# Multiplying half-seen blocks of probabilities at half width, and one group per head in a windowed attention

## Chip, cores and metric

The kernel runs on one core of a Trainium2 chip. The metric is the device time of one execution in microseconds. The engines are named as in the profile: PE is TensorE (PEld its weight loads), DVE is VectorE, ACT is ScalarE, POOL is GpSimd, and SP issues most of the transfers.

## What is computed

The reference is one layer of a decoder on 1024 tokens of width 1024: three attentions side by side, A, B and C, whose outputs are gated and merged, and then an MLP. What matters here is what each attention multiplies with the values:

```python
# A, per head: two softmaxes, their difference, all earlier keys
w = p[0] - lam * p[1]
return jnp.einsum('bhqk,bkhe->bqhe', w, v)
# B: a window of 128 keys, 8 heads, 2 key/value heads
mask = ((dist >= 0) & (dist < window)) & (k_pos >= 0)
o = jnp.einsum('bngrqk,bnkgd->bngrqd', p, vb)
# C: three softmaxes, of compressed keys, of selected blocks (here all), of a window of 512
out = g[..., 0:1] * o_cmp + g[..., 1:2] * o_sel + g[..., 2:3] * o_win
```

Tokens and keys are cut into tiles of 128, eight of each. In A and in the selected part of C, token tile t sees key tiles 0 to t; in B it sees t - 1 and t; in the window of C it sees t - 4 to t.

## The kernel before

Every product of two float32 matrices is made of float32r halves: a high part and a low part are split off by ACT (L90, the copy that rounds) and by DVE or POOL (L91, the difference), and TensorE multiplies two or three times with them (mm3, L114 to L120; head_values in B and C, L901 and L902).

The work of A, B and C is made from two streams. The fine stream is the attention itself. It works on items: in A one head and one pair of token tiles (2qb, 2qb+1), in B two heads and one pair, in C one head and one pair. An item has rows (logits on TensorE at L711, the minimum on DVE at L735, the exponential on ACT at L743, the scaling at L941 in B and L1046 in C) and groups. A group transposes blocks of probabilities on TensorE (L759) into one PSUM tile of 512 columns, splits them into ph and pl (pblocks, L745), and two groups later multiplies them with the values (values, for A, or head_values). All products of one item and head go into one PSUM tile, ac, 256 columns wide, 128 for each token tile; there is a single one of it. When the last product is in, ACT and DVE evict it (L907 and L908, tiles ot and ob; L889 in A), and the next head's first product waits for that.

The dense stream is the projection of the next head, the gates, or the first branch: long runs of 384 or 512 columns wide multiplies that need no attention result. The function mix lays the two streams into TensorE's order: each fine step returns an estimate of its TensorE time and of its DVE time, and dense steps are put in until the sum of TensorE's estimates has reached what DVE's are worth (PACE and STEP are the factors). The order on TensorE is the one so written; the other engines' orders are made by a scheduler.

A group holds two key tiles (in B one or two, see below), each for two token tiles, so four blocks of 128 columns. Where a key tile is seen by one token tile only, its other block is zero: POOL writes zeros into ph and pl (L756, L757) and the multiply runs over all 256 columns. The order of the key tiles within the tile is chosen (order, L772) so that the written blocks lie side by side. B's pairs have three key tiles from the second pair on, 2qb-1, 2qb and 2qb+1, which the kernel before handles as two groups per head: one of key tile 2qb-1 alone (one block and a zero block) and one of the other two.

Of the kernel before, what the change touches and what calls it, by code (L numbers as in the profile page):

```python
# [11 lines left out]
F32 = mybir.dt.float32  # L12
# [5 lines left out]
P = 128  # L18
# [57 lines left out]
class Kernel:  # L76
# [668 lines left out]
    def pblocks(self, blocks):  # L745

        nc, at = self.nc, self.at
        ph = at.tile([P, 512], F32R, name="ph", tag="ph", bufs=self.dist)
        pl = at.tile([P, 512], F32R, name="pl", tag="pl", bufs=self.dist)  # L750
        pt = self.tr()
        rows = blocks[0][0].shape[-1]
        used = sorted(o for _, o in blocks)
        for o in range(0, used[-1] + (2 * P if used[-1] % (2 * P) == 0 else P), P):
            if o not in used:
                nc.gpsimd.memset(ph[0:rows, o:o + P].bitcast(F32), 0.0)  # L756
                nc.gpsimd.memset(pl[0:rows, o:o + P].bitcast(F32), 0.0)  # L757
        for src, o in blocks:
            nc.tensor.transpose(pt[0:rows, o:o + P], src, self.ident)  # L759
        s = slice(used[0], used[-1] + P)  # L760
        assert used == list(range(s.start, s.stop, P))
        with self.tc.high_priority(offset=self.urgent):
            self.split(ph[0:rows, s], pl[0:rows, s], pt[0:rows, s])
        return ph, pl

    def group(self, prow, qb, kts, vis, values):

        out = {}
        see = [[j for j in range(2) if vis(2 * qb + j, kt)] for kt in kts]  # L770

        order = sorted(range(len(kts)), key=lambda i: (see[i] == [0], see[i] != [1]))  # L772
        blocks = [(i, j, (2 * x + j) * P) for x, i in enumerate(order) for j in see[i]]

        def tp():
            out["p"] = self.pblocks([(prow(j, kts[i]), o) for i, j, o in blocks])
            return 0.11 * len(blocks)

        def pv():
            ph, pl = out["p"]  # L780
            c = 0.0
            for i in range(len(kts)):
                s = slice(order.index(i) * 256, order.index(i) * 256 + 256)
                c += values(i, ph[:, s], pl[:, s])
            return c

        return tp, pv

    def items_a(self, h, sta):
        nc, at = self.nc, self.at  # L790
        bias = self.bias[:, h, :]
        for qb in range(4):
            pq = [None, None]
            box = {}
# [58 lines left out]
            def values(i, ph, pl, kt, qb=qb, box=box):  # L853
                if kt + i == 0:
                    box["ac"] = self.ac()
                self.mm3(box["ac"], sta["v"][:, kt + i, 0, :], sta["v"][:, kt + i, 1, :], ph, pl,
                         kt + i == 0, kt + i == 2 * qb + 1)
# [6 lines left out]
            groups = [self.group(lambda j, kt, pq=pq: pq[j][:, kt * P:(kt + 1) * P], qb, (kt, kt + 1),  # L864
                                 lambda t, kt: kt <= t, lambda i, ph, pl, kt=kt, values=values: values(i, ph, pl, kt))
# [28 lines left out]
    def head_values(self, box, dst, v, ph, pl, first, last):  # L894
# [6 lines left out]
        nc.tensor.matmul(ac, v, ph, start=first, stop=False)  # L901
        nc.tensor.matmul(ac, v, pl, start=False, stop=last)  # L902
# [9 lines left out]
    def items_b(self, g, sta):  # L912
        nc, at = self.nc, self.at
        bias = self.bias
        for qb, r0 in [(qb, r0) for qb in range(4) for r0 in (0, 2)]:
# [31 lines left out]
            kts = list(range(max(2 * qb - 1, 0), 2 * qb + 2))  # L947
            box = {}
            for i in range(2):
                def prow(j, kt, i=i, pq=pq):  # L950
                    p, k0 = pq[j]
                    return p[:, i, (kt - k0) * P:(kt - k0 + 1) * P]

                r = r0 + i
                dst = self.od[4 + 2 * g + r // 2, (r % 2) * 64:(r % 2) * 64 + 64, qb * 256:(qb + 1) * 256]
                for grp in ([kts] if len(kts) == 2 else [kts[0:1], kts[1:3]]):
                    def values(i, ph, pl, grp=grp, kts=kts, box=box, dst=dst):
                        kt = grp[i]
                        return self.head_values(box, dst, sta["v"][:, kt, :], ph, pl, kt == kts[0], kt == kts[-1])

                    groups.append(self.group(prow, qb, grp, lambda t, kt: t - 1 <= kt <= t, values))
            yield dict(rows=rows, groups=groups, end=[])

    def items_c(self, g, sta):
        nc, at = self.nc, self.at
        bias4 = self.bias
        for r in range(4):
            for qb in range(4):
# [82 lines left out]
                for j in range(2):  # L1051
# [13 lines left out]
                hv = lambda v, ph, pl, first, last, dst=dst, box=box: self.head_values(  # L1065
                    box, dst, v, ph, pl, first, last)
                blk = {}

                def tp_c(rows=rows, blk=blk):
                    blk["p"] = self.pblocks([(rows[j][0], j * P) for j in range(2)])  # L1070
                    return 0.22

                def pv_c(blk=blk, hv=hv):
                    ph, pl = blk["p"]
                    return hv(self.vct[:, g, :], ph[:, 0:256], pl[:, 0:256], True, False)

                groups = [(tp_c, pv_c)]
                for kt in range(0, 2 * qb + 2, 2):
# [3 lines left out]
                        lambda i, ph, pl, kt=kt, hv=hv: hv(sta["vs"][:, kt + i, :], ph, pl, False, False)))  # L1082
                for kt in range(max(2 * qb - 4, 0), 2 * qb + 2, 2):
# [3 lines left out]
                        lambda i, ph, pl, kt=kt, hv=hv, qb=qb: hv(sta["vw"][:, kt + i, :], ph, pl, False,  # L1087
                                                                  kt + i == 2 * qb + 1)))
# [500 lines left out]
```

## Time and profile before

| what | value |
|---|---|
| median of 3 runs | 2041.63 us (2040.56 to 2045.64) |
| profiled execution | 2045.69 us |
| its span | 2043.7 us, granted clock 0.98 |
| attention A, B, the two halves of C | 147 to 436, 436 to 558, 627 to 870, 917 to 1194 us |
| blocks of probabilities transposed (L759) | 792 of p, 64 of pc, in 280 evictions |
| multiplies into ac | 240 in A, 848 in B and C |
| memsets of ph and pl on POOL | 152 and 152 |

The span runs from the first to the last instruction; the execution's own time has 2.0 us around it. In a group of the profile stand the line, the engine, the operation, the tiles (out<-in), the shape and the count, then the busy time in us, the mean of one in ns, the engine's idle time just before them and what ended most of that. A matmul is pipelined with the next, so its length is not what it costs: the cost is the step from its start to the next one's. A line such as "POOL ph L756 <- PE ac L901" in the waits says which instructions waited for which, with the total, the number of times and the longest.

### The profile page before, as it was taken

How to read it: one execution, taken by the hardware profiler on the slowest of the kernel's cores; microseconds unless marked ns; L12 is line 12 of the kernel's file. 1: busy time of each engine (PE TensorE's matmuls, PEld its weight loads, DVE VectorE, ACT ScalarE, POOL GpSimd, SP SyncE). 2: the span in 40 equal slices, each digit the busy share in tenths (PEclk: the TensorE clock that was granted, in tenths of full speed). 3: DMA queues.
4: the chain of work that ended last, by engine and by line, in shares of the span. 5: the costliest groups of instructions: out<-in, count | busy, mean ns of one | idle time of the engine just before them, and what ended most of it. 6: DMA issues, size and time to landing. Idle time of an engine off the chain costs nothing. (4 is left out here: it accounts for less than half of the span.)

```text
span 2043.7 us, 30701 instructions
## 1 busy us (share of the span) xinstructions
PE 1901.7 (93%) x9838; PEld 1621.5 (79%) x9838; DVE 1423.4 (70%) x3231; ACT 1022.0 (50%) x2626; POOL 954.3 (47%) x1142
## 2 busy tenths in 40 slices
PE   7999888988799999999999899999899998999998
PEld 6888887888688888887888677787688886888876
DVE  6757777788848677648676755657755544889898
ACT  5456556666636555536555533335455544444331
POOL 4455355544352212162222227218444445789784
PEclk9999999999999999999999899999899998999999
DMA  5131022011211111212242456425444446355343
GB/s 218 51 104 52 4 55 59 26 38 37 87 28 61 56 52 51 72 33 91 68 147 77 159 198 204 147 93 161 172 167 160 144 145 247 119 167 163 124 144 114
DMA packets 122558, 219.49 MB, mean 107 GB/s; under 512 B 14420, under 2 KB 35412, under 8 KB 122396
## 3 DMA queue, kind: packets, MB, share of 16 engines
q1 hardware_dynamic: 120812, 211.75, 31.9%
q10 hardware_dynamic: 1584, 5.77, 0.9%
q8 instruction: 78, 1.28, 0.3%
q14 instruction: 84, 0.69, 0.1%
HBM read 156.59 MB, written 64.81 MB: 108 GB/s over the span
## 5 line engine op out<-in xcount | busy, mean ns | idle before, releaser
L91 POOL TENSOR_TENSOR wl<-wr,wh 128x512 fp32r<-128x512 f32 (+3 forms) x246 | 328.8, 1343 | 275.0 <-ACT wh L90 238.8
L90 ACT ACTIVATE wh<-wr 128x512 fp32r<-128x512 f32 (+3 forms) x258 | 150.3, 590 | 183.8 <-PE mm L119 124.1
L711 PE MATMUL sc<-st 128*128 128x256 f32 (+5 forms) x736 | 183.9, 344 | 25.9 <-ACT p L743 25.3
L90 ACT ACTIVATE ph<-tr 128x384 fp32r<-128x384 f32 (+3 forms) x280 | 138.4, 497 | 105.5 <-PE tr L759 87.0
L91 DVE TENSOR_TENSOR pl<-tr,ph 128x384 fp32r<-128x384 f32 (+3 forms) x280 | 155.8, 559 | 40.2 <-ACT ph L90 37.6
L756 POOL MEMSET ph<- 128x128 f32 x152 | 35.7, 235 | 291.3 <-PE ac L901 253.0
L711 PEld LDWEIGHTS sc<-st 128*128 128x128 f32 x736 | 122.8, 192 | 47.5 <-ACT p L743 38.8
L118 PE MATMUL mm<-hh,wh 128*128 128x512 f32 x384 | 158.8, 414 | 0.0
L120 PE MATMUL mm<-hh,wl 128*128 128x512 f32 x384 | 151.5, 395 | 0.0
L119 PE MATMUL mm<-hl,wh 128*128 128x512 f32 x384 | 151.4, 394 | 0.0
L119 PE MATMUL mm<-wl,wh 128*128 128x512 f32 x352 | 139.5, 396 | 9.4 <-POOL wl L91 9.4
L118 PE MATMUL mm<-wh 128*128 128x512 f32 x352 | 139.9, 398 | 8.2 <-DVE x L1471 5.3
L90 ACT ACTIVATE wh<-u 128x512 fp32r<-128x512 f32 x162 | 93.0, 620 | 106.3 <-PE mm L119 27.9
L759 PE MATMUL tr<-ident,p 128*128 128x128 f32 x792 | 129.2, 275 | 16.9 <-ACT o L889 7.8
L120 PE MATMUL mm<-wh,wl 128*128 128x512 f32 x352 | 139.1, 395 | 0.0
L743 ACT ACTIVATE p<-sc,mc 128x256 f32<-128x256 f32 (+5 forms) x200 | 106.7, 538 | 52.0 <-DVE mc L735 47.0
L901 PE MATMUL ac<-ph,st 128*128 128x256 f32 x392 | 109.8, 298 | 19.4 <-DVE ob L908 11.5
L91 POOL TENSOR_TENSOR wl<-s,wh 128x512 fp32r<-128x512 f32 x64 | 89.5, 1405 | 79.3 <-ACT wh L90 79.3
L118 PE MATMUL mm<-wh,hh 128*128 128x384 f32 (+1 forms) x320 | 117.0, 366 | 0.0
L91 DVE TENSOR_TENSOR wl<-u,wh 128x512 fp32r<-128x512 f32 x98 | 112.5, 1150 | 3.9 <-ACT wh L90 3.9
L902 PE MATMUL ac<-pl,st 128*128 128x256 f32 x392 | 106.5, 292 | 6.5 <-DVE pl L91 5.8
L91 POOL TENSOR_TENSOR wl<-u,wh 128x512 fp32r<-128x512 f32 x64 | 98.8, 1557 | 25.1 <-ACT wh L90 25.0
(311 smaller groups left out, 5771.2 us busy)
## 6 DMA issues: line engine op xcount, KB each, us to landing
ud<-u SPq DMA_DIRECT2D x112, 256.0 KB, 2.2
u<-ud SPq DMA_DIRECT2D x98, 256.0 KB, 3.3
wr<-wu SPq DMA_DIRECT2D x76, 256.0 KB, 2.8
wr<-wd SPq DMA_DIRECT2D x64, 256.0 KB, 2.9
gd<-go SPq DMA_DIRECT2D x48, 256.0 KB, 2.0
g<-gd SPq DMA_DIRECT2D x48, 256.0 KB, 3.2
wr<-wg SPq DMA_DIRECT2D x40, 256.0 KB, 2.7
wr<-wbr SPq DMA_DIRECT2D x40, 256.0 KB, 3.0
```

The lines of the kernel that those rows point to most:

```text
L90: nc.scalar.activation(hi, src, AF.Copy)
L91: (eng or nc.vector).tensor_tensor(lo, src, hi.bitcast(F32), op=ALU.subtract)
L118: mm(out, lh, rh, start=first, stop=False, skip_group_check=more)
L119: mm(out, lh, rl, start=False, stop=False, skip_group_check=more)
L120: mm(out, ll, rh, start=False, stop=last, skip_group_check=more)
L711: self.nc.tensor.matmul(ps[:, off:off + k1 - k0], q[:, t * P:(t + 1) * P], k[:, k0:k1], start=i == 0, stop=i == 1)
L743: self.nc.scalar.activation(p, ps, AF.Exp, bias=m, scale=-1.0, accum_out=l)
L756: nc.gpsimd.memset(ph[0:rows, o:o + P].bitcast(F32), 0.0)
L759: nc.tensor.transpose(pt[0:rows, o:o + P], src, self.ident)
L901: nc.tensor.matmul(ac, v, ph, start=first, stop=False)
L902: nc.tensor.matmul(ac, v, pl, start=False, stop=last)
```

## The change

Blocks are laid into the PSUM tile one after the other, without places for zero blocks, and the memsets go. A group remembers for each key tile which token tiles see it (js); the multiply takes only these columns of ph and pl and adds them into the same columns of ac. In B a head from the second pair on has one group of four blocks, with the key tiles in the order 2qb, 2qb+1, 2qb-1, so that the first multiply covers all 256 columns. The estimate of a narrow multiply is halved.

```diff
     def pblocks(self, blocks):
...
-        for o in range(0, used[-1] + (2 * P if used[-1] % (2 * P) == 0 else P), P):
-            if o not in used:
-                nc.gpsimd.memset(ph[0:rows, o:o + P].bitcast(F32), 0.0)
-                nc.gpsimd.memset(pl[0:rows, o:o + P].bitcast(F32), 0.0)
-        for src, o in blocks:
-            nc.tensor.transpose(pt[0:rows, o:o + P], src, self.ident)
+        n = len(blocks) * P
+        for i, src in enumerate(blocks):
+            nc.tensor.transpose(pt[:, i * P:(i + 1) * P], src, self.ident)
         with self.tc.high_priority(offset=self.urgent):
-            self.split(ph[0:rows, s], pl[0:rows, s], pt[0:rows, s])
+            self.split(ph[:, 0:n], pl[:, 0:n], pt[:, 0:n])
...
     def group(self, prow, qb, kts, vis, values):
...
         def pv():
             ph, pl = out["p"]
-            c = 0.0
-            for i in range(len(kts)):
-                s = slice(order.index(i) * 256, order.index(i) * 256 + 256)
-                c += values(i, ph[:, s], pl[:, s])
+            c, o = 0.0, 0
+            for i, js in enumerate(see):
+                s = slice(o * P, (o + len(js)) * P)
+                c += values(i, ph[:, s], pl[:, s], slice(js[0] * P, (js[-1] + 1) * P)) * len(js) / 2
+                o += len(js)
             return c
...
     def head_values(self, box, dst, v, ph, pl, js, first, last):
...
-        nc.tensor.matmul(ac, v, ph, start=first, stop=False)
-        nc.tensor.matmul(ac, v, pl, start=False, stop=last)
+        nc.tensor.matmul(ac[:, js], v, ph, start=first, stop=False, skip_group_check=True)
+        nc.tensor.matmul(ac[:, js], v, pl, start=False, stop=last, skip_group_check=True)
...
     def items_b(self, g, sta):
...
-            kts = list(range(max(2 * qb - 1, 0), 2 * qb + 2))
+            kts = [2 * qb, 2 * qb + 1, 2 * qb - 1][0:3 if qb else 2]
...
-                for grp in ([kts] if len(kts) == 2 else [kts[0:1], kts[1:3]]):
-                    def values(i, ph, pl, grp=grp, kts=kts, box=box, dst=dst):
-                        kt = grp[i]
-                        return self.head_values(box, dst, sta["v"][:, kt, :], ph, pl, kt == kts[0], kt == kts[-1])
-
-                    groups.append(self.group(prow, qb, grp, lambda t, kt: t - 1 <= kt <= t, values))
+
+                def values(i, ph, pl, js, kts=kts, box=box, dst=dst):
+                    kt = kts[i]
+                    return self.head_values(box, dst, sta["v"][:, kt, :], ph, pl, js, kt == kts[0], kt == kts[-1])
+
+                groups.append(self.group(prow, qb, kts, lambda t, kt: t - 1 <= kt <= t, values))
```

A's values and C's calls hand js through in the same way, so their last key tiles (and the first of C's window from the third pair on) are multiplied at 128 columns.

On TensorE, near the end of B, one head's turn in the kernel before is this (ac is its accumulator, tr the PSUM tile that blocks of the probabilities p are transposed into, two groups ahead of their use; ident is the identity, st holds the values):

```order
L901 MATMUL ac_6701<-ph_6627,st_4990 128x256
L902 MATMUL ac_6701<-pl_6628,st_4990 128x256
L759 MATMUL tr_6706<-ident_98,p_6496 128x128
L901 MATMUL ac_6701<-ph_6691,st_4990 128x256
L902 MATMUL ac_6701<-pl_6692,st_4990 128x256
L901 MATMUL ac_6701<-ph_6691,st_4990 128x256
L902 MATMUL ac_6701<-pl_6692,st_4990 128x256
L759 MATMUL tr_6723<-ident_98,p_6526 128x128
L759 MATMUL tr_6723<-ident_98,p_6496 128x128
L759 MATMUL tr_6723<-ident_98,p_6526 128x128
```

With the change the same place on TensorE reads:

```order
L892 MATMUL ac_6630<-ph_6539,st_4960 128x256
L893 MATMUL ac_6630<-pl_6540,st_4960 128x256
L892 MATMUL ac_6630<-ph_6539,st_4960 128x128
L893 MATMUL ac_6630<-pl_6540,st_4960 128x128
L892 MATMUL ac_6630<-ph_6539,st_4960 128x128
L893 MATMUL ac_6630<-pl_6540,st_4960 128x128
L754 MATMUL tr_6644<-ident_98,p_6441 128x128
L754 MATMUL tr_6644<-ident_98,p_6462 128x128 x2
L754 MATMUL tr_6644<-ident_98,p_6441 128x128
```

The six multiplies of a head now stand together, four of them 128 wide, and the four transposes of a later head follow them as one tile, where before two tiles were filled, the first in the midst of the head.

On DVE, in the same stretch, the eviction ob of an accumulator stands between the minimum steps of the rows (L735 with its read of the accumulated minimum), the splits pl and the steps on lb that make the scale of a row. Before:

```order
L735 ISA sc_6999,mb_7002<-sc_6999,bias_6263,sink_212 128x256
L735 ISA mb_7002 128x1
L908 TENSOR_TENSOR ob_7028<-ac_6988,ot_7027 64x256
L91 TENSOR_TENSOR pl_7033<-tr_7034,ph_7032 128x384
L936 TENSOR_TENSOR lb_7001<-sink_212,mb_7002 128x2
L938 TENSOR_TENSOR lb_7001<-lb_7001 128x2
L91 TENSOR_TENSOR pl_7046<-tr_7047,ph_7045 128x128
L939 RECIPROCAL lb_7001<-lb_7001 128x2
L941 TENSOR_SCALAR p_7000<-p_7000,lb_7001 128x256 x2
L908 TENSOR_TENSOR ob_7058<-ac_7042,ot_7057 64x256
```

With the change, on DVE:

```order
L735 ISA sc_6772,mb_6775<-sc_6772,bias_6121,sink_212 128x256
L735 ISA mb_6775 128x1
L927 TENSOR_TENSOR lb_6753<-sink_212,mb_6754 128x2
L927 TENSOR_TENSOR lb_6774<-sink_212,mb_6775 128x2
L899 TENSOR_TENSOR ob_6804<-ac_6796,ot_6803 64x256
L91 TENSOR_TENSOR pl_6809<-tr_6810,ph_6808 128x512
L929 TENSOR_TENSOR lb_6753<-lb_6753 128x2
L929 TENSOR_TENSOR lb_6774<-lb_6774 128x2
L930 RECIPROCAL lb_6753<-lb_6753 128x2
L899 TENSOR_TENSOR ob_6825<-ac_6817,ot_6824 64x256
```

One split of 512 columns stands where one of 384 and one of 128 stood, and the steps of two rows (6753 and 6774, the two token tiles of an item) run side by side ahead of the eviction, where they came one row after the other.

On POOL, in C, the memsets of the blocks of probabilities stand among the splits wl of the gates' weights wr. Before:

```order
L757 MEMSET pl_10115 128x128
L91 TENSOR_TENSOR wl_10529<-wr_10527,wh_10528 128x512
L756 MEMSET ph_10223 128x128
L757 MEMSET pl_10224 128x128
L756 MEMSET ph_10236 128x128
L757 MEMSET pl_10237 128x128
L91 TENSOR_TENSOR wl_10535<-wr_10533,wh_10534 128x512
```

With the change only the splits of weights are left there on POOL:

```order
L91 TENSOR_TENSOR wl_7935<-wr_7933,wh_7934 128x512
L91 TENSOR_TENSOR wl_7941<-wr_7939,wh_7940 128x512
L91 TENSOR_TENSOR wl_8182<-wr_8180,wh_8181 128x512
L91 TENSOR_TENSOR wl_8188<-wr_8186,wh_8187 128x512
L91 TENSOR_TENSOR wl_8425<-wr_8423,wh_8424 128x512
```

Nothing of the attention stands between them any more.

More of the change, by code (lines that the diff above doesn't have):

```diff
@@ L770, in group @@
         see = [[j for j in range(2) if vis(2 * qb + j, kt)] for kt in kts]
-        order = sorted(range(len(kts)), key=lambda i: (see[i] == [0], see[i] != [1]))
-        blocks = [(i, j, (2 * x + j) * P) for x, i in enumerate(order) for j in see[i]]
         def tp():
-            out["p"] = self.pblocks([(prow(j, kts[i]), o) for i, j, o in blocks])
-            return 0.11 * len(blocks)
+            out["p"] = self.pblocks([prow(j, kt) for js, kt in zip(see, kts) for j in js])
+            return 0.11 * sum(map(len, see))
         def pv():
             ph, pl = out["p"]
-            c = 0.0
-            for i in range(len(kts)):
-                s = slice(order.index(i) * 256, order.index(i) * 256 + 256)
-                c += values(i, ph[:, s], pl[:, s])
+            c, o = 0.0, 0
[3 more added lines that the diff above has]
+                o += len(js)
             return c
@@ L851, in items_a, with values @@
                     rows.append(lambda c=c, mem=mem, own=own, t=t, j=j, f=near: f(c, mem, own, t, j))
-            def values(i, ph, pl, kt, qb=qb, box=box):
+            def values(i, ph, pl, js, kt, qb=qb, box=box):
                 if kt + i == 0:
                     box["ac"] = self.ac()
-                self.mm3(box["ac"], sta["v"][:, kt + i, 0, :], sta["v"][:, kt + i, 1, :], ph, pl,
-                         kt + i == 0, kt + i == 2 * qb + 1)
+                self.mm3(box["ac"][:, js], sta["v"][:, kt + i, 0, :], sta["v"][:, kt + i, 1, :], ph, pl,
+                         kt + i == 0, kt + i == 2 * qb + 1, True)
                 if kt + i == 2 * qb + 1:
@@ L892, in items_a, with head_values @@
             yield dict(rows=rows, groups=groups, end=[by_token])
-    def head_values(self, box, dst, v, ph, pl, first, last):
+    def head_values(self, box, dst, v, ph, pl, js, first, last):
         nc, at = self.nc, self.at
@@ L1064, in items_c @@
                 dst = self.od[8 + 2 * g + r // 2, (r % 2) * 64:(r % 2) * 64 + 64, qb * 256:(qb + 1) * 256]
-                hv = lambda v, ph, pl, first, last, dst=dst, box=box: self.head_values(
-                    box, dst, v, ph, pl, first, last)
+                hv = lambda v, ph, pl, js, first, last, dst=dst, box=box: self.head_values(
+                    box, dst, v, ph, pl, js, first, last)
                 blk = {}
                 def tp_c(rows=rows, blk=blk):
-                    blk["p"] = self.pblocks([(rows[j][0], j * P) for j in range(2)])
+                    blk["p"] = self.pblocks([rows[j][0] for j in range(2)])
                     return 0.22
```

14 lines of the change are left out of this document (5 added, 9 removed).

## Prediction

> **What bounds the kernel now.** I read the page first, then the busy times of the three attention stretches that the change touches, then the groups and the waits of each stretch, and last TensorE's order of time, for the price of one multiply.
>
> ```profile
> span 2043.7 us, 30701 instructions
> ...
> PE 1901.7 (93%) x9838; PEld 1621.5 (79%) x9838; DVE 1423.4 (70%) x3231; ACT 1022.0 (50%) x2626; POOL 954.3 (47%) x1142
> ```
>
> The stretches, one row each:
>
> ```profile
> 147.00:436.00 289.00, 257.61 (x1621) 239.07 (x1620) 220.81 (x623) 174.88 (x576) 143.05 (x221) 0.98 0.14 39
> 436.00:558.00 122.00, 102.51 (x652) 91.76 (x651) 105.35 (x368) 82.31 (x283) 49.09 (x147) 0.97 0.20 56
> 627.00:870.00 243.00, 232.78 (x1361) 201.38 (x1360) 173.82 (x562) 141.59 (x398) 48.49 (x101) 1.00 0.18 57
> 917.00:1194.00 277.00, 254.20 (x1434) 217.35 (x1433) 205.50 (x641) 159.95 (x451) 69.84 (x125) 0.98 0.33 103
> 1130.00:1194.00 64.00, 50.29 (x268) 41.54 (x267) 47.48 (x139) 33.69 (x93) 15.12 (x28) 0.89 0.35 113
> ```
>
> Each has start and end, length, then the busy time of PE, weight loads, DVE, ACT and POOL. 147 to 436 is attention A, 436 to 558 B, the next two the two halves of C; the last row is the end of C, where the dense multiplies that fill TensorE have run out. A and C are TensorE's (89%, 96%, 92%). B is not: DVE is busy 105.35 of 122 us, TensorE 102.51, and a busy TensorE counts the overlapping ends of its multiplies. So a saving on TensorE counts in A and C, a saving on VectorE in B, and after 1194 us nothing changes.
>
> **Narrower multiplies.** By the code, a key tile that only one token tile sees is multiplied 128 columns wide in place of 256. A has 4 heads x 4 pairs x 3 multiplies = 48 of these, B 8 heads x 7 x 2 = 112, C 8 heads x 10 x 2 = 160 (per head one selected and one window tile in each of four pairs, and one more in the last two): 320. Their price is the step to the next start, which TensorE's order of time gives: start, length, line, shape.
>
> ```profile
> 999.41 0.28 PE L901 MATMUL ac<-ph,st 128*128 128x256 f32 x1
> ...
> 999.88 0.49 PE L759 MATMUL tr<-ident,p 128*128 128x128 f32 x3
> ```
>
> ```profile
> 121.58 0.28 PE L120 MATMUL sc<-wh,yl 128*128 128x64 f32 x1
> ...
> 122.03 0.48 PE L118 MATMUL mm<-hh,wh 128*128 128x512 f32 x1
> ```
>
> ```profile
> 452.60 0.45 PE L558 MATMUL tr<-identr,tm 128*128 128x128 f32 x4
> 452.89 0.35 PE L901 MATMUL ac<-ph,st 128*128 128x256 f32 x1
> ```
>
> And the groups of weight loads (busy, mean ns):
>
> ```profile
> L759 PEld LDWEIGHTS tr<-ident,p 128*128 128x128 f32 x792 | 92.4, 141 | 22.1 <-ACT o L889 10.4 <-DVE pl L91 6.2 <-DVE st L564 4.6
> ...
> L901 PEld LDWEIGHTS ac<-ph,st 128*128 128x128 f32 x392 | 74.7, 190 | 28.6 <-issue 7.4 <-POOL st L91 7.2 <-POOL pl L757 6.2
> ```
>
> A 256-wide multiply steps (999.88 - 999.41) / 4 = 118 ns, there being four between the first row and the last. A 64-wide one, a quarter of the columns, still steps (122.03 - 121.58) / 4 = 112 ns: the next weight load sets it, not the columns. So a narrow multiply with another multiply behind it saves only 118 - 112 = 6 ns. Where transposes stand behind it the load is the shorter one (141 ns against 190), and four 128-wide transposes step (452.89 - 452.60) / 4 = 73 ns: there I take 118 - 73 = 45 ns. In the changed order 108 of the 320 stand ahead of transposes (16 in A, 30 in B, 62 in C), 212 ahead of a multiply (32, 82, 98). A: 32 x 6 + 16 x 45 = 0.9 us; B: 82 x 6 + 30 x 45 = 1.8; C: 98 x 6 + 62 x 45 = 3.4. The ends are all at 6 ns (1.9 us in all) and all at 45 (14.4).
>
> The Trainium skill (TensorE: Matmul & The Clock Gate, section "LDWEIGHTS (loading the stationary operand)") says that a load takes its columns over 1.2 GHz, thus 107 ns for 128, which speaks against the change; the 112 ns step agrees, and an estimate from that page alone would be 320 x (118 - 107) = 3.5 us.
>
> **One group per head in B.** In B 24 heads (8 heads, in three of the four pairs of token tiles) lose their second eviction of probabilities: one 512-wide split stands in place of a 128-wide and a 384-wide one. The scale of the probabilities on DVE (L941) is also slower when a memset runs beside it.
>
> Busy us and mean ns of the groups of B on DVE:
>
> ```profile
> L735 DVE CUSTOM_DVE_ANT_0 sc<-sc,bias,sink 128x256 f32<-128x256 f32 x49 | 23.6, 486 | 5.6 <-ACT p L743 3.1 <-PE sc L711 1.8
> L941 DVE TENSOR_SCALAR p<-p,lb 128x256 f32<-128x256 f32 x52 | 20.8, 440 | 0.3
> L91 DVE TENSOR_TENSOR pl<-tr,ph 128x384 fp32r<-128x384 f32 x28 | 15.4, 549 | 1.6 <-ACT lb L937 0.6 <-ACT ph L90 0.5
> ...
> L91 DVE TENSOR_TENSOR pl<-tr,ph 128x128 fp32r<-128x128 f32 x23 | 6.5, 281 | 1.7 <-ACT ph L90 1.5
> ```
>
> Then the 512-wide split over the whole span, L941 with its shortest, middle and longest instance, and one wait of B (total us, times, longest):
>
> ```profile
> L91 DVE TENSOR_TENSOR pl<-tr,ph 128x512 fp32r<-128x512 f32 x96 | 65.8, 685 | 22.1 <-ACT ph L90 21.2 <-issue 0.2
> ```
>
> ```profile
> L941 DVE TENSOR_SCALAR p<-p,lb x56: 279/348/1291, 437.1 to 556.5; 128x256 f32<-128x256 f32 x52, 128x128 f32<-128x128 f32 x4
> ```
>
> ```profile
> PE ac L901 <- DVE ob L908: 10.1, 9, 2.0
> ```
>
> Splits: 24 x (549 + 281 - 685) = 3.5 us of DVE. Scaling: the mean is 440 ns and the median 348, so 52 x (440 - 348) = 4.8 us is what some instances wait, and I charge that to the memsets. Together 8.3 of 105.35 us. B stands between the two engines: none of it counts if TensorE's wait for the single accumulator (L901 for ob, 10.1 us) stays what ends last; then B gains TensorE's 1.8. All of it and TensorE's 1.8 would be 10.1. I take 5.5, nearer to the DVE row, DVE being 86% busy. Late next is that accumulator wait: each head still evicts it before the next may begin.
>
> The Trainium skill (SBUF — State Buffer, section "SBUF: two separate sides") says that GpSimd and VectorE share one port pair under an exclusive lock, the loser blocked for the whole instruction. An estimate by it, with every memset of B in the way of a VectorE instruction, is some 100 x 0.22 = 22 us of VectorE time; the L941 rows show 4.8.
>
> **The memsets.** 304 leave POOL (us, mean ns, idle before them).
>
> ```profile
> L756 POOL MEMSET ph<- 128x128 f32 x152 | 35.7, 235 | 291.3 <-PE ac L901 253.0 <-DVE lc L1042 8.7 <-DVE mc L728 8.1
> L757 POOL MEMSET pl<- 128x128 f32 x152 | 34.3, 226 | 6.9 <-PE ac L119 6.5
> ```
>
> TensorE's largest dense group (its last number is its idle time), the waits in C, and one of B:
>
> ```profile
> L118 PE MATMUL mm<-hh,wh 128*128 128x512 f32 x384 | 158.8, 414 | 0.0
> ```
>
> ```profile
> PE sc L711 <- ACT p L743: 15.1, 16, 3.2
> ...
> ACT ph L90 <- POOL pl L757: 6.3, 9, 1.5
> ```
>
> ```profile
> ACT ph L90 <- POOL ph L756: 4.8, 9, 0.9
> ```
>
> They hold POOL's queue for 70.0 us of work and 298 us of waiting, and the weight splits queue behind them. That looks large and I cost it at nothing: the dense multiplies that need those weights have waited 0.0 us, so the weights come early enough already. SP's loads of raw weights start earlier with POOL free; DMA is 14 to 33% busy there. ACT's waits for a memset (6.3 us in C, 4.8 in B) sit two groups ahead of the multiply that uses the block, so I cost them at nothing too; where that cover is missing they add up to 6.3 us to the gain, which the low end of the range holds. TensorE's own wait in C is for the logits' banks (15.1 us), which the change does not touch.
>
> **The order.** The estimates that place dense multiplies fall with the narrow ones, so up to 18 dense multiplies come earlier in C; the same number is left at each stage's end. That costs nothing by itself. But in B, 15 of the 16 items (two heads, one pair of token tiles) now issue both tokens' logits ahead of the multiplies that stand beside them, where the second stood between two heads' halves (rival two).
>
> **Sum.** A 0.7 (0.9 less a fifth, as TensorE is busy 89% there and some narrow ones end at a wait), B 5.5, C 3.0 (3.4 less an eighth, for the stretch 1130 to 1194, in which TensorE idles 14 us anyway): 9.2 us. The profiled execution took 2045.69 us, its span and 2.0 around it: 2036.5. The median of the runs shown, 2041.63, is 0.2% under that execution: 2032.
>
> **Rivals.**
> 1. *Hidden.* The load sets every step, transposes included, and B's accumulator wait takes what DVE gives: 1.9 us, 2040 on the scale of the median. For it: the 112 ns step, the 10.1 us. Against: DVE's 86%. 0.28.
> 2. *Slower by bunching in B.* Both tokens' minimum steps (L735) now stand in DVE's queue ahead of the accumulator's eviction ob. One more token is 2 x 486 ns = 0.97 us, and if dense work covers none of it, 15 items pay 14.6 us: the gain of 9.2 becomes a loss of 5.4, 2047. It decides if ob waits over 0.6 us more per item than now (9.2 / 15). Against: dense multiplies stand between the logits and the multiplies, in which DVE can get through. 0.07.
> 3. *A narrow multiply costs more per column.* If 128 columns took what 512 take,
>
> ```profile
> 611.06 0.36 PE L711 MATMUL sc<-st 128*128 128x192 f32 x2
> 611.26 0.42 PE L118 MATMUL mm<-hh,wh 128*128 128x512 f32 x1
> 611.52 0.39 PE L119 MATMUL mm<-hl,wh 128*128 128x512 f32 x1
> 611.75 0.40 PE L120 MATMUL mm<-hh,wl 128*128 128x512 f32 x1
> ```
>
> the step would be 230 ns (611.75 - 611.52) and the loss 320 x 112 = 36 us, some 2074. Against: two 192-wide multiplies took 0.20 us together. 0.02.
> 4. *The columns alone count.* If all 320 step like the transposes, 73 ns: A 2.2, C 7.2, B 5.5, 14.9 us, 2027. Against: the 64-wide rows. 0.05. The Trainium skill (TensorE: Matmul & The Clock Gate, section "Back-to-back issue gap") has such a rule, columns over 2.4 GHz and 2.5 ns, for isolated multiplies: 56 ns at 128 columns, by estimate 320 x 62 = 20 us.
>
> **How the numbers follow.** The forecast has 0.58, with a gain of 6.5 to 14 us of its own (2027 to 2035). About 0.3%, 6 us, is what a measurement of this kernel can tell from no change: faster by more is the forecast and rival four, 0.63; within it rival one, 0.28; slower rivals two and three, 0.09. The range 2024 to 2042 takes in the forecast, rival four and most of rival one.
>
> **What would show it.** Right: 128-wide multiplies stepping 110 to 115 ns, 60 to 85 ahead of transposes; L941's successor with a mean near 350 ns; B 116 us or so; C's halves 1 to 2 us shorter each; POOL's memset rows gone and TensorE's dense rows still at 0.0 idle. Wrong: B as long as before with a larger accumulator wait (rival one or two), or narrow multiplies over 118 ns (rival three).

## The result and the profile after

The changed kernel is slower: 2056.06 us (2050.78 to 2062.84, 6 runs) against 2041.1 us (2039.71 to 2045.77, 6 runs), a ratio of 1.0068 [1.0047, 1.0089], about 14 us. The forecast was 2032, and no rival gave this time by this cause. The execution in the trace took 2062.84 us, the longest of the six.

The head of the page after:

```profile
span 2061.1 us, 30035 instructions
...
PE 1901.0 (92%) x9838; PEld 1622.2 (79%) x9838; DVE 1418.2 (69%) x3207; ACT 1020.2 (49%) x2602; POOL 891.0 (43%) x838
```

TensorE has as many instructions as before and as much busy time, though 320 of its multiplies are narrower. POOL has 304 fewer, the memsets, and no memset of ph or pl is left in its groups. The 17.4 us by which the span grew must lie in waits and in the clock, whose slow stretches count as busy time. The stretches of the prediction, moved to where they now lie (busy time of PE, weight loads, DVE, ACT, POOL, then the granted clock):

```profile
145.00:445.00 300.00, 261.46 (x1620) 241.95 (x1619) 224.08 (x627) 175.50 (x578) 138.03 (x187) 0.97 0.14 38
445.00:571.00 126.00, 106.05 (x668) 95.06 (x667) 101.64 (x344) 79.95 (x260) 30.67 (x46) 0.92 0.20 55
637.00:880.00 243.00, 227.07 (x1331) 198.13 (x1329) 172.85 (x558) 140.99 (x396) 29.81 (x23) 0.99 0.19 62
927.00:1207.00 280.00, 257.59 (x1465) 220.80 (x1463) 204.08 (x645) 162.71 (x455) 58.86 (x51) 0.98 0.33 103
```

A lost most. From here on a stage is measured from the start of its first product into ac to the start of its last (in A, of the last product's first multiply):

| kernel | A (half clock) | B (half clock) | C (half clock) | after C |
|---|---|---|---|---|
| before | 267.8 (10.2) | 125.6 (7.9) | 567.0 (13.7) | 849.7 |
| after | 279.6 (20.5) | 125.3 (19.5) | 569.3 (13.7) | 854.3 |

In brackets are the us of the stage in which the granted clock was 0.5. It comes in pieces of 3.41 us. Most of the 4.6 us behind C is scatter: in the other traces without added multiplies that stretch takes 848.9 to 853.8 us, whatever the order ahead of it. TensorE's waits in A, with total, number and longest, after:

```profile
PE sc L711 <- ACT p L743: 12.4, 13, 1.9
PE tr L878 <- DVE st L564: 8.1, 3, 4.7
```

And before:

```profile
PE sc L711 <- ACT p L743: 7.4, 10, 1.7
...
PE tr L887 <- DVE st L564: 3.2, 3, 1.1
```

The logits (sc) wait 5.0 us more for a free bank, and the transposes of A's output (L878) 4.9 us more for the cast L564, most of it in one wait of 4.7 us. The place where the logits' wait shows most plainly is the first pair of token tiles of every head of A. TensorE before, at the first head (start, length, line, shape, and the wait ahead in brackets):

```profile
172.39 0.60 PE L759 MATMUL tr<-ident,p 128*128 128x128 f32 x4
172.74 0.42 PE L118 MATMUL mm<-wh,hh 128*128 128x384 f32 x1
...
173.35 0.62 PE L711 MATMUL sc<-st 128*128 128x512 f32 x2
...
175.85 0.45 PE L558 MATMUL tr<-identr,tm 128*128 128x128 f32 x4
176.14 0.70 PE L711 MATMUL sc<-st 128*128 128x512 f32 x2
...
177.56 0.73 PE L711 MATMUL sc<-st 128*128 128x512 f32 x2 [0.20 <-ACT p L743]
```

The same place after:

```profile
170.92 0.60 PE L754 MATMUL tr<-ident,p 128*128 128x128 f32 x4
171.27 0.71 PE L711 MATMUL sc<-st 128*128 128x512 f32 x2
...
173.86 0.45 PE L558 MATMUL tr<-identr,tm 128*128 128x128 f32 x4
174.16 0.70 PE L711 MATMUL sc<-st 128*128 128x512 f32 x2
...
177.23 0.73 PE L711 MATMUL sc<-st 128*128 128x512 f32 x2 [1.85 <-ACT p L743]
```

Three dense multiplies (mm) that stood between the transposes and the first logits have gone to an earlier place. From the transposes to the fourth logits it was 177.56 - 172.39 = 5.17 us and is now 177.23 - 170.92 = 6.31. Why the earlier logits do not end earlier stands in VectorE's rows, before:

```profile
174.59 0.69 DVE L725 TENSOR_REDUCE m<-sc 128x1 f32<-128x512 f32 x1
175.19 0.42 DVE L727 TENSOR_REDUCE m<-sc 128x1 f32<-128x256 f32 x1
...
176.15 0.48 DVE L735 CUSTOM_DVE_ANT_0 sc<-sc,bias,m 128x256 f32<-128x256 f32 x1
176.55 0.14 DVE L735 DVE_READ_ACCUMULATOR2_ANT m<- 128x1 f32 x1
176.55 0.69 DVE L564 CAST st<-tr 128x512 fp32r<-128x512 f32 x1
177.15 0.68 DVE L725 TENSOR_REDUCE m<-sc 128x1 f32<-128x512 f32 x1
```

And after:

```profile
172.47 0.68 DVE L725 TENSOR_REDUCE m<-sc 128x1 f32<-128x512 f32 x1
...
173.99 0.41 DVE L727 TENSOR_REDUCE m<-sc 128x1 f32<-128x256 f32 x1
174.36 0.69 DVE L564 CAST st<-tr 128x512 fp32r<-128x512 f32 x1
...
175.03 0.68 DVE L725 TENSOR_REDUCE m<-sc 128x1 f32<-128x512 f32 x1
...
175.81 0.49 DVE L735 CUSTOM_DVE_ANT_0 sc<-sc,bias,m 128x256 f32<-128x256 f32 x1
```

A row's minimum is taken in three parts, L725, L727 and L735, and ACT's exponential, which frees the bank, waits for the last. L564 is the eviction of the dense stream's own transposes (tr<-identr,tm). With the dense stream three multiplies further, its transposes come 2.94 us behind those of p, not 3.46. Before, the row's three parts ran ahead of L564 and of the next row's L725 (a row has one, so the second in each list is the next row's). After, the first part starts sooner behind the transposes of p (1.55 us, not 2.20), but L564 and the next row's L725, 0.60 us each to the next start, stand ahead of the last part, which starts 4.89 us behind them, not 3.76. The same wait stands at this place in every head: 1.85, 1.67, 1.67 and 1.85 us, where before none of the four was over 0.6. The five traces here with a halved estimate in A and no added multiplies have these four waits to within 0.01 us, and the six with a whole one have none over 0.6.

C lost by other waits. TensorE's in C, after:

```profile
PE sc L711 <- ACT p L743: 12.0, 12, 2.2
PE ac L892 <- DVE ob L899: 11.9, 9, 3.9
PE ac L893 <- DVE pl L91: 10.7, 17, 1.5
```

And in the kernel with the estimate left whole, whose experiment comes first below:

```profile
PE sc L711 <- ACT p L743: 14.3, 18, 2.8
PE ac L892 <- DVE ob L899: 9.4, 10, 1.9
PE ac L893 <- DVE pl L91: 4.5, 11, 1.2
```

There the logits wait less, and the products wait 6.2 us more for the splits of the probabilities and 2.5 us more for the accumulator. What in the order brings this about was not followed row by row.

Behind such a wait can come a slow stretch of the clock. Four stretches of 3.41 us around the one of the third head, after (length, busy time of PE with its instructions, ..., granted clock):

```profile
319.22:322.64 3.42, 3.42 (x21) 3.21 (x22) 2.92 (x9) 1.32 (x6) 2.47 (x5) 1.00 0.11 38
322.64:326.05 3.41, 1.74 (x11) 1.34 (x10) 2.10 (x6) 1.08 (x3) 0.27 (x1) 1.00 0.00 0
326.05:329.46 3.41, 3.41 (x12) 3.11 (x12) 1.85 (x6) 1.79 (x7) 0.00 (x0) 0.50 0.00 0
329.46:332.87 3.41, 3.41 (x25) 3.38 (x25) 2.41 (x6) 3.17 (x10) 1.99 (x2) 1.00 0.00 0
```

In the second, TensorE was idle for half; the third ran at half clock and got 12 instructions done, the fourth 25. The Trainium skill (TensorE: Matmul & The Clock Gate, section "Part 1: The HAM clock gate") says that the clock is decided by free-running windows of 3413 ns, and these rows have that length. The Trainium skill (TensorE: Matmul & The Clock Gate, section "HAM oscillation — how this bites in real kernels") gives the rule that no idle gap be over about 3.4 us; here a wait of 1.67 us was enough.

### The profile page after: what moved, and what is told of

Read it like the earlier page. It is cut to its first block, busy times and chain, and to the rows that moved or that the text cites. A ratio compares the mean times of both kernels' runs of the same rounds, so it can differ in the third digit from the quotient of the medians.

```text
span 2061.1 us, 30035 instructions
## 1 busy us (share of the span) xinstructions
PE 1901.0 (92%) x9838; PEld 1622.2 (79%) x9838; DVE 1418.2 (69%) x3207; ACT 1020.2 (49%) x2602; POOL 891.0 (43%) x838
## 5 line engine op out<-in xcount | busy, mean ns | idle before, releaser
L711 PE MATMUL sc<-st 128*128 128x256 f32 (+5 forms) x736 | 182.7, 343 | 27.4 <-ACT p L743 27.3
L90 ACT ACTIVATE ph<-tr 128x384 fp32r<-128x384 f32 (+2 forms) x256 | 134.4, 528 | 99.9 <-PE tr L754 92.3
L91 DVE TENSOR_TENSOR pl<-tr,ph 128x384 fp32r<-128x384 f32 (+2 forms) x256 | 152.4, 598 | 40.3 <-ACT ph L90 38.2
L711 PEld LDWEIGHTS sc<-st 128*128 128x128 f32 x736 | 125.3, 193 | 48.5 <-ACT p L743 37.8
L892 PE MATMUL ac<-ph,st 128*128 128x256 f32 (+1 forms) x392 | 104.1, 286 | 21.5 <-DVE ob L899 17.5
L533 POOL TENSOR_TENSOR y<-raw 128x256 f32<-128x256 f32 (+2 forms) x64 | 50.6, 793 | 140.4 <-ACT raw L520 135.4
L893 PE MATMUL ac<-pl,st 128*128 128x256 f32 (+1 forms) x392 | 101.2, 294 | 10.9 <-DVE pl L91 10.7
L119 PE MATMUL mm<-wl,hh 128*128 128x384 f32 (+1 forms) x320 | 111.2, 347 | 0.0
```

Of the source, the lines that this page charges most:

```text
L90: nc.scalar.activation(hi, src, AF.Copy)
L91: (eng or nc.vector).tensor_tensor(lo, src, hi.bitcast(F32), op=ALU.subtract)
L119: mm(out, lh, rl, start=False, stop=False, skip_group_check=more)
L533: nc.gpsimd.tensor_tensor(y[:, 0:nn, :], x, x, op=ALU.mult)
L711: self.nc.tensor.matmul(ps[:, off:off + k1 - k0], q[:, t * P:(t + 1) * P], k[:, k0:k1], start=i == 0, stop=i == 1)
L892: nc.tensor.matmul(ac[:, js], v, ph, start=first, stop=False, skip_group_check=True)
```

## The experiments

Theories at the start: E, the halved estimate, by the order that it makes; C, the clock; P, POOL that runs ahead without its memsets. Each is timed beside the kernel before on the same chip, and its ratio is to that.

**The estimate whole.** The changed kernel with

```diff
-                c += values(i, ph[:, s], pl[:, s], slice(js[0] * P, (js[-1] + 1) * P)) * len(js) / 2
+                c += values(i, ph[:, s], pl[:, s], slice(js[0] * P, (js[-1] + 1) * P))
```

> The whole change, but the estimate that lays out the dense stream is not halved for a narrow multiply, so that TensorE's order in A and C, and with it nearly all of VectorE's and ScalarE's order there, is that of the kernel before. Theory E (the estimate: moved dense multiplies leave attention A with longer waits for exponentials and casts): A, from its first to its last product with the values, goes back from 280 us to 265 to 268, and the whole is 3 to 10 us under the kernel before. Theory C (the clock: multiplies without zero blocks leave TensorE less active, so its clock is halved more often): still 8 to 15 us over the kernel before, with six or more half-clock windows in A. Theory P (POOL without memsets runs ahead and its weight splits get in the way): still 8 to 15 us over.

2032.22 us, ratio 0.997 [0.9956, 0.9985]: 6 us faster than before, and some 20 under the changed kernel, with all of its multiplies narrow and no memsets. E holds (A takes 263.0 us, even under its 265), P falls, and so does C as it stood there, with narrow multiplies as the cause of the whole loss. No other kernel here is clearly faster. Its waits in A:

```profile
PE sc L711 <- ACT p L743: 6.0, 10, 1.6
...
PE tr L878 <- DVE st L564: 3.2, 3, 1.2
```

**One stage at a time.** Only one attention is changed (with halved estimates); the others keep wide multiplies, zero blocks and whole estimates.

```diff
     def group(self, prow, qb, kts, vis, values):
+        if not self.narrow:
+            return self.group_wide(prow, qb, kts, vis, values)
```

> The change in attention A alone (narrow multiplies, no memsets, halved estimate); B and C as before. Theory E, theory C and theory P all expect A at about 280 us in place of 268, and 8 to 12 us over the kernel before; if it is within 3 us of before, the loss does not come from A's own instructions.

> The change in B alone (narrow multiplies, one group per head, no memsets, halved estimate there); A and C keep every engine's order. My forecast's own term: 5.5 us under the kernel before. Theory C: 0 to 5 us over, with more half-clock windows in B. Rival two of the prediction (bunching): 5 us over or more, with a longer wait of the multiplies for the accumulator's eviction.

> The change in C alone (narrow multiplies, no memsets, halved estimate there); A and B keep every engine's order. My forecast's own term: 3 us under the kernel before. Theory E: 0 to 4 us over, C waiting longer for exponentials or splits. Theory C: over, with more half-clock windows than the two stretches of the kernel before near 1134 and 1151 us.

A alone 1.0041 [1.0026, 1.0056], B alone 0.9971 [0.9957, 0.9985], C alone 1.0008 [0.9996, 1.002]: +8, -6 and +2 us. So the part for B brings what was forecast for it, A loses, and C, not clearly slower, lacks the 3 us that were forecast for it.

**The estimate alone, and by stage.** The kernel before with `* len(see[i]) / 2` and nothing else; the changed kernel with the estimate halved in B alone; in B and C alone; and at 1.5 in place of 0.5 (`* (2 - len(js) / 2)`).

> The kernel before with one thing of the change only: the estimate that a multiply of a half-seen key tile returns is halved, in A, B and C. All multiplies stay 256 wide, the zero blocks and their memsets stay, B keeps its two groups per head. Theory E (the halved estimate, by the order that it makes, is what costs; the narrow multiplies and B's single group gain about 6 us whatever the order): the changed kernel lies 20 us (ratio 1.0068 against 0.997) above the one with whole estimates, so here before plus 15 to 25 us, ratio 1.007 to 1.012, A over 276 us from its first to its last product into ac. Theory N (the order is harmless with wide multiplies, which cover the waits for TensorE; it costs only with narrow ones): within 4 us of before, ratio 0.998 to 1.002.

> The changed kernel with the estimate halved in B only, whole in A and C. Theory E1 (the halving hurts in A and C, where TensorE is the bound, and is harmless in B): A and C as with whole estimates (263 and 561 us), B as in the kernel with B's part alone (121 us or less), 2028 to 2032 us, ratio 0.994 to 0.997. Theory E2 (it hurts in all three): 2034 to 2040, slower than with whole estimates everywhere by 2 us or more, with B at 126 us or over.

> The changed kernel with the estimate whole in A alone, halved in B and C. Measured so far: whole everywhere -6 us against before, whole in A and C -5, halved everywhere +14. Theory D (A and C each have their own share; from the parts alone A's halving costs about 9 us and C's about 5): 2043 to 2047 us, ratio 1.002 to 1.004, with A at 263 to 268 us from first to last product and C near 569. Theory J (the two halvings cost more together than apart, so that one of them taken back takes back nearly all): 2034 to 2040, ratio under 1.0005.

> The changed kernel with the estimate of a half-seen key tile at one and a half instead of a half: dense multiplies then stand later than in the kernel before (up to 3 in A, 18 and 33 in the two halves of C), where the halved estimate has them earlier by up to 6, 18 and 18. Theory M (the more dense work is held back for the stage's end, the better): 2026 to 2032 us, ratio under 0.996. Theory T (PACE and STEP were set for whole estimates, and every shift of the dense multiplies, either way, takes cover from waits that were covered): slower than with whole estimates by 3 to 15 us, 2035 to 2047, with TensorE idle over 33 us in A or C and more than 30 us of half clock from A to the end of C.

| kernel | median us | ratio to before | A (half clock) | B | C (half clock) |
|---|---|---|---|---|---|
| wide, halved | 2053.84 | 1.0071 [1.0053, 1.0089] | 275.3 (17.1) | 121.0 | 569.6 (13.7) |
| narrow, halved in B | 2034.19 | 0.9975 [0.9963, 0.9986] | 267.7 (10.2) | 122.4 | 559.3 (6.8) |
| narrow, halved in B and C | 2042.51 | 1.0019 [1.0008, 1.003] | 263.8 (3.4) | 122.6 | 570.3 (20.5) |
| narrow, whole | 2032.22 | 0.997 [0.9956, 0.9985] | 263.0 (0) | 125.3 | 561.0 (10.2) |
| narrow, at 1.5 | 2049.23 | 1.0057 [1.0042, 1.0073] | 269.7 (6.8) | 118.4 | 578.1 (34.1) |

The halved estimate alone, with every multiply as wide as before, costs as much as the whole change: E holds in time (A, at 275.3, is just under its 276), and theory N (harmless with wide multiplies) falls. It also means that in the halved order the narrow multiplies and B's single group bring nothing that can be measured (1.0068 against 1.0071), where E had counted on 6 us whatever the order. Whole in A takes back 1.0068 - 1.0019, 10 us, whole in C as well another 9, and in B it makes no difference to the time (0.9975 against 0.997). 0.9975 lies just over E1's range, with E2's time but not its B of 126 us or over; 1.0019 lies just under D's range and outside J's. Holding the dense multiplies back instead (at 1.5) loses too: theory T, by 2 us more than it said, not M. C is then the longest of all, and its waits for the logits' banks are 20.2 us against 14.3 with whole estimates. The point at which the dense stream stood was better than either of the two that were tried around it.

**A and B together, and memsets kept.** The changed kernel with C as before, and the changed kernel with memsets into columns that nothing reads:

```diff
         n = len(blocks) * P
+        if n % 256:
+            nc.gpsimd.memset(ph[:, n:n + P].bitcast(F32), 0.0)
+            nc.gpsimd.memset(pl[:, n:n + P].bitcast(F32), 0.0)
```

> The changed kernel with C as before: A and B narrow, with halved estimates and B's single group, C wide with its zero blocks and whole estimates. A's and B's orders on VectorE are those of the changed kernel row for row. Parts alone measured A +8, B -6, C +2 us, 4 together, where the whole measured +14. Theory S (they add; the missing 10 us are the half-clock windows that a run happens to get): +2 us, ratio 0.999 to 1.003. Theory J (B loses its gain when A's order stands ahead of it, or A loses more with B's steps mixed into its end): +8 to +12, ratio 1.004 to 1.006, with A near 280 us and B at 125 rather than 121.

> The changed kernel with memsets of zeros kept on GpSimd, two for every group of blocks that is not a multiple of 256 columns wide, into columns that nothing reads; the narrow multiplies, the single group in B and the halved estimate are as in the changed kernel. Theory P (GpSimd without memsets runs ahead, and its splits and what they start collide with VectorE or the transfers): back to before or under it, 2036 to 2042 us, ratio 0.997 to 1.001. Theory E: as slow as the changed kernel, 2052 to 2062, ratio 1.005 to 1.010, a little more if the memsets themselves cost.

Memsets kept (208 of them; in B only those of the first pair are left, as the other groups are full): 1.0085 [1.0067, 1.0103], as slow as the changed kernel. P falls a second time. A and B together: 1.005 [1.0034, 1.0066], +10 us where the two alone add up to +2.5. That is J's ratio, but not J's cause: its trace has A at 275.1, as in A alone, and B at 122.8, nearly as short as in B alone. What makes the runs of this combination longer than the sum is open; the intervals are some 3 us wide to each side and explain only part of it.

**Does the clock follow the waits?** Multiplies that do no work were laid ahead of 42 of TensorE's instructions that waited 0.5 us or more in two traces of this order, 2 to 16 at each.

```diff
+    def ahead(self):
+        for _ in range(FILL.get(self.count, 0)):
+            k.nc.tensor.matmul(k.dm[:, 0:64], k.identr, k.hh[:, 0, 0:64], start=True, stop=True)
+        self.count += 1
```

> The changed kernel with 273 multiplies of 64 columns added, into a part of the accumulator's bank that nobody reads: they stand ahead of 42 of TensorE's instructions that waited 0.5 us or more in two traces of this order (not ahead of those that wait for the accumulator itself), so many at each that at 118 ns a step they end 0.25 us before the wait did. They do no work of the result. VectorE's order moves a little, by its scheduler (144 of 756 rows in A). Theory C (a good half of the loss is the half clock that follows the waits): half clock from A's first product to C's last, 58 us in the changed kernel's profile, falls below 35 us, and the time by 6 to 14 us, to 2042 to 2050, though work is added. Theory W (the waits alone are the loss, and the clock follows something else): the waits are only filled, so 2054 to 2062, with 50 us of half clock or more.

> The changed kernel with whole estimates, and 277 such multiplies of 64 columns ahead of 51 instructions that waited 0.5 us or more in its trace. Theory C: half clock from A to the end of C, 27 us in its profile, falls below 15 us, and the time by 3 to 8 us, to 2024 to 2029, ratio 0.993 to 0.9955, the fastest so far. Theory W: 2031 to 2038, ratio 0.997 to 0.999.

1.022 [1.0201, 1.024] and 1.0174 [1.0155, 1.0193], far outside both theories. These two say nothing of either: the count was off by two, so the added multiplies stood behind the instructions that wait. (They share the accumulator's bank, whose sums are not kept in these kernels.) Straight ahead of the waiting instructions, at three widths:

> The changed kernel with the same 273 multiplies of 64 columns, now straight ahead of the 42 waiting instructions (in the run before, a count was off and they stood two instructions behind them, where they could fill no wait). They write into the accumulator's bank beside it, so the products of the attentions are not kept. Theory K (the clock of each stretch of 3413 ns is set by the columns that TensorE streamed in the stretch before, and 64 columns in a step of 112 ns are 27 ns of streaming): the waits are filled and the half clock stays, 45 us or more from A's first to C's last product, 2050 to 2062, ratio 1.005 to 1.010. Theory I (any instruction keeps the clock, as long as TensorE doesn't idle): half clock under 35 us, 2042 to 2050.

> The same with 128 columns to each added multiply, at the same places and in the same order. Theory K: 128 columns are 53 ns of a step of about 112, half the stretch, over the third at which the clock stayed full: half clock under 35 us from A to the end of C, 2040 to 2050. Theory I: as with 64 columns, within 4 us. Theory W (the clock doesn't follow the waits at all): half clock as in the changed kernel, near 58 us, 2052 to 2064, whatever the width.

> The same with 256 columns, 107 ns of streaming in a step of 118. Theory K: the half clock that follows these 42 waits goes, under 25 us from A to the end of C, 2036 to 2048, ratio 0.999 to 1.004, A from first to last product 265 to 270 us where the changed kernel's profile has 279.6. Theory I: as with 64 columns. Theory W: 2052 to 2064.

> The changed kernel with whole estimates and 277 added multiplies of 256 columns straight ahead of 51 instructions that waited 0.5 us or more in its trace. Theory K: half clock from A to the end of C from 27 us to under 15, 2022 to 2030, ratio 0.992 to 0.996. Theory W: 2030 to 2036, ratio 0.996 to 0.9985.

| kernel | median us | ratio | TensorE idle in A | half clock in A | half clock, A to end of C |
|---|---|---|---|---|---|
| after | 2056.06 | 1.0068 [1.0047, 1.0089] | 38.0 | 20.5 | 58.1 |
| 64 columns | 2064.18 | 1.0123 [1.011, 1.0136] | 21.9 | 23.9 | 64.9 |
| 128 columns | 2056.69 | 1.0084 [1.0069, 1.0099] | 21.9 | 6.8 | 34.1 |
| 256 columns | 2052.4 | 1.0058 [1.0046, 1.007] | 21.2 | 0 | 30.7 |

A of the kernels with 64, 128 and 256 columns, one view each; the figure to read is the granted clock, third from the end:

```profile
160.00:440.00 280.00, 258.08 (x1654) 244.00 (x1654) 205.87 (x567) 162.82 (x534) 130.33 (x173) 0.96 0.14 41
```

```profile
158.00:433.00 275.00, 253.08 (x1660) 238.18 (x1659) 206.78 (x568) 162.90 (x535) 130.11 (x173) 0.99 0.15 41
```

```profile
160.00:434.00 274.00, 252.78 (x1660) 236.36 (x1659) 206.95 (x570) 162.84 (x534) 130.60 (x173) 1.00 0.15 41
```

The instructions and their places are the same in the three, TensorE's idle time in A nearly so, and with the columns alone the half clock in A goes from 23.9 us to none. It isn't one trace's luck: the mean granted clock, as the median of all runs of each, is 0.973, 0.9775 and 0.980. I (any instruction keeps the clock) falls, and so does W's clock (58 us of half clock whatever the width). K holds for the clock with 64 and 128 columns; with 256, 30.7 us were left, not under 25, and 22.7 of them in B. For the time K was too hopeful each time: 2064.18, 2056.69 and 2052.4, where it said at most 2062, 2050 and 2048; the last two lie where W had them. With whole estimates the same fillers made the kernel slower, 2047.27 us, 1.0037 [1.0023, 1.0051], and left 37.5 us of half clock where 27.3 had been. In that kernel 277 fillers of 120 ns are 33 us of TensorE, and its waits from A to C fell by 21: fillers are no cure.

How much of the loss is the clock? The changed kernel and the one with whole estimates have the same multiplies. In the traces the first takes 27.0 us longer from A's first to C's last product (1046.8 and 1019.8). TensorE is idle for 13.8 us more in it; the other 13.2 are busy time, with 30.7 us more of half clock, 0.43 for each. So about half is the clock and half the waits themselves. This division is worked out, not shown by a run of its own, and the price of half clock differs with the place: between the traces with 64 and 256 columns, 34.2 us of it went and 11.6 us of the way from A to the end of C, 0.34 for each, and in A of the order before, two traces of the same instructions differ by 6.8 us of it and 4.1 us of time, 0.60. The runs are like the traces: their mean granted clock (medians) is 0.973 after and 0.981 with whole estimates, and twice the difference times the span is 33 us of half clock.

## Why the prediction was wrong

**The step that failed** is "The order": the halved estimate's earlier dense multiplies, of which it said "That costs nothing by itself", because as many were left at each stage's end. The count was nearly right (by the traces up to 6 earlier in A, 18 in C's first half, and 30 at one place of its second), the price was not: 14 us by itself (wide, halved), 20 with the narrow multiplies. The forecast asked whether dense work was left at the end. What counted was where it stood. In A: three multiplies fewer ahead of the logits, the dense stream's eviction and the next row's first minimum ahead of a row's last on VectorE, a wait of 1.7 to 1.9 us, and half clock behind it. In C: longer waits for the splits, whose own cause stays open.

**A, 0.7 us.** Too small to be told. With whole estimates A's traces average 264.8 us with narrow multiplies (263.0, 267.7, 263.8) and 265.7 with wide ones (267.8, 263.7, 265.5), 0.9 less, but they scatter by over 4; halved, all five that were traced without added multiplies lie between 274.5 and 279.6.

**C, 3.0 us.** In the traces more than forecast: with whole estimates C averages 560.2 narrow (561.0, 559.3) and 565.2 wide (567.0, 566.7, 563.9, 563.3). "Halves 1 to 2 us shorter each" came true there only; halved and narrow it is 569.3 to 572.3. The runs' times don't bear it out. B alone (0.9971 [0.9957, 0.9985]) and "narrow, halved in B" (0.9975 [0.9963, 0.9986]) differ in the narrow multiplies and memsets of A and C alone, for which 3.7 us were forecast, and the second is no faster, though the intervals leave room for some 3 us. Its mean granted clock is lower (0.9795 against 0.982, medians), 10 us of half clock. At 0.34 to 0.60 these cost 3 to 6 us, about what the traces of the two stages save. Narrow multiplies stream fewer columns, which would fit theory K; no run tests that.

**The price of a narrow step** was put in the wrong places. Two narrow multiplies and what follows, after:

```profile
1000.78 0.28 PE L893 MATMUL ac<-pl,st 128*128 128x256 f32 x1
1000.90 0.22 PE L892 MATMUL ac<-ph,st 128*128 128x128 f32 x1
1000.96 0.28 PE L893 MATMUL ac<-pl,st 128*128 128x128 f32 x1
1001.07 0.62 PE L754 MATMUL tr<-ident,p 128*128 128x128 f32 x4
```

The first steps 0.06 us, though a multiply stands behind it, and the second 0.11, though transposes do: the opposite of the assignment. Over the trace the medians are 61 and 113 ns, 174 for a pair where two wide ones take 236, so 31 ns saved for each, between the 6 and the 45 of the prediction. (These are the pairs of B and C; A's three multiplies step 58, 112 and 112 ns, 24 saved for each.) By the medians the 320 save 9.6 us, against the 6.1 that it summed before its deductions.

**B, 5.5 us.** The kernel with B's part alone gained 5.9 by the median, but the working does not stand. L941's successor, with its number and mean:

```profile
L932 DVE TENSOR_SCALAR p<-p,lb 128x256 f32<-128x256 f32 x50 | 18.2, 402 | 0.3
...
L91 DVE TENSOR_TENSOR pl<-tr,ph 128x512 fp32r<-128x512 f32 x24 | 16.4, 683 | 5.1 <-ACT ph L90 4.9
```

The 24 splits of 512 columns came as computed. The scaling's mean is 402 ns, not 350, while its median stayed (345): of the 4.8 us charged to the memsets 52 x (440 - 402) = 2.0 went. The charge was mostly put on the wrong neighbour. Sorted by what ran on POOL at the same time, the 56 scalings of 128x256 before took 342 ns on average with POOL idle (20 of them), 370 beside a memset alone (14) and 562 beside one of POOL's tensor operations, such as the splits (22); after, 344 (39) and 515 (17). The slow ones stood beside work that the change leaves there. The stage itself is shorter by less than 5.5 in the traces: 126.6 us on average with two groups (125.6, 127.0, 127.1), 122.9 with one group and the halved estimate (125.3, 122.4, 122.6, 121.2, 122.8). Whether the halved estimate is a part of this gain stays open: with two groups, wide and halved, B took 121.0 us, and with one group and whole estimates 125.3, but the times of whole and halved in B are the same. The wait for the accumulator grew, as the prediction feared in its first two rivals, from 10.1 us at this line to

```profile
PE ac L892 <- DVE ob L899: 17.5, 14, 4.3
```

without making B longer: 125.3 after against 125.6 before, with 11.6 us more of half clock in it. The growth is 0.5 us for each of 15 items, under the 0.6 at which rival two would have decided, and B's part alone is faster, so neither rival decided.

**The memsets, nothing.** Right as far as tested: with 208 kept, for which ACT waits 8.6 us in sum (12.2 before), nothing changes that can be measured, and after, without them, the dense rows still wait 0.0:

```profile
L118 PE MATMUL mm<-hh,wh 128*128 128x512 f32 x384 | 161.1, 420 | 0.0
```

**The sum.** With the failing step taken out the forecast of 9.2 us stands against 6 measured (0.997), between the forecast and rival one. Of the rivals, one (hidden), three (more per column) and four (columns alone) are contradicted by the 174 ns of a pair; the chances left no room for a loss by the order. That 6 is near 9.2 is in part luck: B's part alone gave those 6 already, its price was mostly charged to the wrong neighbour, and the terms of A and C don't show in the times.

## What to carry to other kernels

An estimate that only places other work is part of the schedule: making it truer, without setting again the factors that were fitted to the old one, can cost more than the change it describes gains, so time the change with the old estimates first. When an order moves, follow the few places where an instruction that another engine waits for now has something ahead of it in its queue, and add the clock's price to the wait. When some instances of an instruction are slow, sort them by what ran beside them before charging the excess to one neighbour. And a sum that leaves out the moved order because counts at the ends agree has left out the largest term.

## What the hardware showed that was not expected

The granted clock of a stretch of 3413 ns follows the columns that TensorE streamed in the stretch before, not whether it had instructions. A few full ones follow lower counts, down to 2,048; stretches in which a record is missing may be among them, so the limit is a region and not a line. So a wait of 1.7 us can cost a second time, and multiplies of 64 columns, at 112 ns a step, do not keep the clock.

The phase of these stretches differs from trace to trace (the first change of the clock comes 21.18 us into the span before and 18.85 after, no whole number of stretches apart), and the half clock in a stage and its time differ with the same instructions: A in the order before took 263.7, 265.5 and 267.8 us with 3.4, 6.8 and 10.2 us of half clock. One trace of a stage can thus be off by some 4 us, which is more than most terms of the forecast.
